# Two weight pieces split by one VectorE operation, from a ring of six places

## The chip, the cores and the metric

The kernel runs on one core of one Trainium2 chip. The metric is the device time of one execution in microseconds (us), the median over the runs shown. The profile tells of one execution, with its own time and its own span (first to last instruction). Engines are called by the names that the profile uses: PE is TensorE, PEld its weight loads, DVE is VectorE, ACT is ScalarE, POOL is GpSimd, and SP is the engine whose queue issues most of the transfers (DMAs).

## The reference, cut to what matters

The reference is a trunk of two decoder layers over 256 tokens of width 2048, in float32. Layer 0 mixes tokens by block-sparse attention, layer 1 by latent attention, and each is followed by the same gated MLP with 5632 inner features:

```python
def conv_glu_ffn(h, w_gate, w_up, conv_w, conv_b, w_down):
    g = h @ w_gate
    g = causal_depthwise_conv(g, conv_w, width=3) + conv_b
    return (jax.nn.silu(g) * (h @ w_up)) @ w_down

x = x + mixer_i(rms_norm(x, attn_norm[i]))
x = x + conv_glu_ffn(rms_norm(x, ffn_norm[i]), ...)
```

All weights are read once from the chip's main memory, 411 MB in all by the profile, and every product has to keep float32 accuracy.

## The kernel before

**Products in parts.** A float32 number is split into a high part (rounded to the format that TensorE multiplies, `fp32r`) and a low part (the rest). A product is three matmuls: high weights by high activations, high weights by low activations, low weights by high activations. Weights are worked on in *pieces* of 128x512 numbers (a few are 128x288 or 128x576). ACT makes the high part of a piece (`whi`, L183, a copy that rounds) and DVE the low part (`wlo`, L184, weight minus high part). PE then runs the piece's matmuls: twelve of 256 columns for a piece whose result has features in the partitions (`feat_major`, L402, L403, L404: four blocks, three matmuls each), six for a token-major piece (L376) and six for a *block* piece (L1181, L1182, L1183).

**The stream.** `Stream` brings the weights. A *unit* is 512 KB, two pieces in most places, in one of `AHEAD_UNITS = 6` buffers `raw`; at the split of unit u's first piece the loads up to unit u + 5 are recorded on SP's queue (L137, L141), the last of them into the buffer of unit u - 1, which it may fill once DVE has read the second piece there. The parts are in buffers of their own, five `whi` and five `wlo` (`AHEAD_PIECES + 1`). The program is one list of *quanta*, one for each piece. Ahead of quantum q it records the split of all pieces up to q + 3, then the matmuls of q, then the side work that hangs on q:

```python
ws.split(q + min(1 + q // 6, AHEAD_PIECES))
f(*args, *ws.take(q))
```

Each engine runs its own instructions in the recorded order. The split of piece i waits until PE has done with piece i - 5, whose buffers it takes. So ACT and DVE can be at most four pieces ahead of PE.

**The gated MLP.** 20 of the 44 feature tiles have their gate and up products from eight ordinary pieces; 24 have their gate products by *blocks*: four tiles together (a group, six groups a layer), in four rounds (kq) of seven block products. The weights for a round are loaded into `xroom` (L1140), which takes the place of the residual stream `xT`, kept in main memory meanwhile. Three of the seven are quarters of the loaded weights, and four are sums of these that DVE forms in `xroom` (`weight_sum`, L1159): t1 and t3, beside each other, are used by the block pieces s = 3 and 4, t2 and t4, beside each other, by s = 5 and 6. t2 and t4 lie where the group before had its result for a transpose by way of main memory (`turn`, L516, L518, L525), so the first t2 of a group waits for that transfer to have read it. Between block pieces stand ordinary pieces: up products and first down products, `BLOCK_EVERY = 2, 1, 1, 1, 2, 1, 1` of them after each.

When the last group is done, SP's queue issues in this place the reload of the down products kept so far (`a_back`, L1113, 2 MB) and of the residual stream (`xT`, L1134, four times 512 KB), between the loads of weight units.

**Side work.** DVE also evacuates the products from PSUM, multiplies, convolves and splits the activations (L1246, L1248, L1261, L1269, L1276); ACT scales, squares, applies the activation function and rounds (L1255, L1266, L1272). The buffers `nsq` (three) take squares for the norms.

Of the kernel before, what the change touches and what calls it, by code (L numbers as in the profile page):

```python
# [42 lines left out]
AHEAD_UNITS = 6  # L43
AHEAD_PIECES = 4

# [3 lines left out]
ROOM = 64  # L49
# [67 lines left out]
class Stream:  # L117
# [3 lines left out]
    def __init__(self, nc, raw_pool, part_pool, units, starts, pieces):  # L121
        self.starts = starts
        self.nc, self.raw_pool, self.part_pool = nc, raw_pool, part_pool
        self.units = units
        self.pieces = pieces
        self.raw, self.parts, self.after = {}, {}, {}
        self.loaded = self.split_to = 0

# [16 lines left out]
    def begin(self, load_x):  # L145
# [3 lines left out]
        ends = {1: 3, 3: 5, 5: 8, 8: 12, 11: 16}  # L149
# [14 lines left out]
    def split(self, upto):  # L164
        while self.split_to < min(upto, len(self.pieces)):
            i = self.split_to
            u, j, n = self.pieces[i]
            if u is None:
                b, c = BY_BLOCK
                w = j()  # L170
            else:
                self.load(u + AHEAD_UNITS)
                w = self.raw[u][:, j * n : (j + 1) * n]
                b, c = self.starts(u, j)
            hi = self.part_pool.tile([P, 512 + ROOM], F32R, name="whi")[:, b : b + max(n, 512)]
            lo = self.part_pool.tile([P, 512 + ROOM], F32R, name="wlo")[:, c : c + max(n, 512)]
            hi_, lo_ = hi[:, :n], lo[:, :n]
            if len(w.shape) == 4:
                hi_, lo_ = (x.rearrange("p (i j f) -> p i j f", i=2, j=2) for x in (hi_, lo_))
            if i == 0:  # L180
                self.nc.vector.tensor_copy(hi_, w)
            else:
                self.nc.scalar.copy(hi_, w)  # L183
            self.nc.vector.tensor_tensor(lo_, w, hi_.bitcast(F32), op=ALU.subtract)  # L184
            self.parts[i] = (hi, lo, n)
            self.split_to += 1
            for f, args in self.after.pop(i, ()):
                f(*args)

# [5 lines left out]
def trunk(ctx: ExitStack, tc: tile.TileContext, a, out):  # L195
# [4 lines left out]
    part_pool = ctx.enter_context(tc.tile_pool(name="parts", bufs=AHEAD_PIECES + 1))  # L200
# [25 lines left out]
    block_pieces = {}  # L226

    def gate_up_units(layer):
# [12 lines left out]
        for kind, *what in tokens:  # L241
            if kind == "block":
                block_pieces[(layer, *what)] = len(pieces)
                pieces.append((None, lambda layer=layer, what=what: blocks[layer].source(*what), 512))
            elif kind == "down":
                if at_ % 2 == 0:
# [6 lines left out]
                    downs_unit = len(units) - 1  # L253
                pieces.append((downs_unit, at_ % 2, 512))
                at_ += 1
            else:
                j, up, kq = what
                if kq % 2 == 0:
                    units.append(per[(2 * j + up) * 2 + kq // 2])
                    plain_unit = len(units) - 1  # L260
# [1637 lines left out]
```

## Time and profile before

| | |
|---|---|
| median of 3 runs | 2047.85 us (2047.83 to 2049.13) |
| the profiled execution | 2048.13 us, its span 2045.9 us |
| granted TensorE clock | 1.000 over the span |
| PE busy | 2037.8 us, 16300 instructions |
| DVE busy | 1660.1 us, 3211 instructions |
| ACT busy | 1290.9 us, 2474 instructions |
| MoBA attention, its output product | 0 to some 370 us |
| gated MLP of layer 0 | some 370 to 1065 us |
| latent attention, its output product | 1065 to some 1330 us |
| gated MLP of layer 1 | some 1330 to 2046 us |

How to read it: the duration of a matmul in the trace overlaps the next one's (a matmul of 256 columns is shown with 277 ns, while the next begins about 113 ns after it), so PE's share of busy time tells that it had something to do, and an idle time of PE is a wait that cost time. A row of the timeline has the start and the duration in us, the engine, the line, the operation, what it writes and reads, how many such operations follow each other, and in brackets the idle time of the engine ahead of it with what ended it. SPq is the queue in which SP issues transfers; their bytes move later. A row of a list of groups has the number of operations, their busy time in us, the mean ns of one, and the idle time ahead of them.

### The profile page before, as it was taken

How to read it: one execution, taken by the hardware profiler on the slowest of the kernel's cores; microseconds unless marked ns; L12 is line 12 of the kernel's file. 1: busy time of each engine (PE TensorE's matmuls, PEld its weight loads, DVE VectorE, ACT ScalarE, POOL GpSimd, SP SyncE). 2: the span in 40 equal slices, each digit the busy share in tenths (PEclk: the TensorE clock that was granted, in tenths of full speed). 3: DMA queues.
4: the chain of work that ended last, by engine and by line, in shares of the span. 5: the costliest groups of instructions: out<-in, count | busy, mean ns of one | idle time of the engine just before them, and what ended most of it. 6: DMA issues, size and time to landing. Idle time of an engine off the chain costs nothing.

```text
span 2045.9 us, 43563 instructions
## 1 busy us (share of the span) xinstructions
PE 2037.8 (100%) x16300; PEld 1970.4 (96%) x16300; DVE 1660.1 (81%) x3211; ACT 1290.9 (63%) x2474; POOL 48.7 (2%) x38
## 2 busy tenths in 40 slices
PE   9999999999999999999999999999999999999999
PEld 7888899999999999999999889999999999999999
DVE  7877777788998888888666998778889888898655
ACT  6656666666666666655556786666666666666443
POOL 0010000000000000000000110000000000000000
PEclk9999999999999999999999999999999999999999
DMA  7777776676766776676655646567666767758664
GB/s 274 235 250 223 226 231 210 211 233 203 225 218 207 237 239 189 223 267 208 199 196 159 210 152 183 189 214 234 207 214 217 227 217 227 225 186 301 202 211 129
DMA packets 162531, 440.35 MB, mean 215 GB/s; under 512 B 18816, under 2 KB 42880, under 8 KB 162064
## 3 DMA queue, kind: packets, MB, share of 16 engines
q1 hardware_dynamic: 162000, 437.21, 66.6%
q8 instruction: 127, 2.08, 0.4%
q14 instruction: 84, 0.69, 0.1%
q10 hardware_dynamic: 288, 0.33, 0.1%
q0 software_dynamic: 32, 0.04, 0.0%
HBM read 411.16 MB, written 26.35 MB: 214 GB/s over the span
## 4 chain that ended last, share of the span: by engine, by line
PE 97%; DVE 2%; ACT 0%; DMA 0%; issue 0%; SPq 0%; DVEq 0%; ACTq 0%
PE acc L404 23%; PE acc L403 22%; PE acc L402 22%; PE acc L376 16%; PE tp L1183 2%; PE tp L1181 2%; PE tp L1182 2%; PE sc L1183 2%; PE sc L1182 2%; PE sc L1181 2%; DVE wlo L184 1%; PE sc L657 0%; PE sc L656 0%; PE sc L655 0%; PE sc L758 0%; DMA xT<-in_xT 0%
## 5 line engine op out<-in xcount | busy, mean ns | idle before, releaser
L183 ACT CAST whi<-raw 128x512 fp32r<-128x512 f32 (+1 forms) x1271 | 775.6, 621 | 437.4 <-PE acc L403 223.4
L184 DVE TENSOR_TENSOR wlo<-raw,whi 128x512 fp32r<-128x512 f32 (+1 forms) x1272 | 861.1, 689 | 199.0 <-ACT whi L183 170.2
L404 PE MATMUL acc<-h,wlo 128*128 128x256 f32 x2112 | 585.3, 277 | 0.5 <-DVE wlo L184 0.5
L402 PE MATMUL acc<-h,whi 128*128 128x256 f32 x2112 | 585.1, 277 | 0.0
L403 PE MATMUL acc<-h,whi 128*128 128x256 f32 x2112 | 585.0, 277 | 0.0
L404 PEld LDWEIGHTS acc<-h,wlo 128*128 128x128 f32 x2112 | 396.5, 188 | 1.5 <-DVE wlo L184 1.4
L403 PEld LDWEIGHTS acc<-h,whi 128*128 128x128 f32 x2112 | 396.5, 188 | 0.0
L402 PEld LDWEIGHTS acc<-h,whi 128*128 128x128 f32 x2112 | 396.5, 188 | 0.0
L183 ACT CAST whi<-xroom 128x512 fp32r<-128x512 f32 x336 | 208.9, 622 | 102.6 <-PE acc L403 76.6
L376 PE MATMUL acc<-whi,h 128*128 128x512 f32 (+1 forms) x896 | 265.7, 377 | 0.9 <-ACT h L424 0.9
L184 DVE TENSOR_TENSOR wlo<-xroom,whi 128x512 fp32r<-128x512 f32 x336 | 231.1, 688 | 18.9 <-ACT whi L183 9.2
L376 PEld LDWEIGHTS acc<-whi,h 128*128 128x128 f32 x896 | 164.8, 188 | 31.1 <-ACT h L424 1.4
L376 PE MATMUL acc<-wlo,h 128*128 128x512 f32 (+1 forms) x448 | 168.8, 377 | 0.3 <-DVE wlo L184 0.2
L402 PE MATMUL acc<-oT,whi 128*128 128x256 f32 x512 | 142.8, 279 | 0.0
L403 PE MATMUL acc<-a_one,whi 128*128 128x256 f32 x512 | 142.0, 277 | 0.0
L404 PE MATMUL acc<-a_one,wlo 128*128 128x256 f32 x512 | 142.0, 277 | 0.0
L402 PE MATMUL acc<-a_one,whi 128*128 128x256 f32 x512 | 141.9, 277 | 0.0
L404 PE MATMUL acc<-oT,wlo 128*128 128x256 f32 x512 | 141.9, 277 | 0.0
L403 PE MATMUL acc<-oT,whi 128*128 128x256 f32 x512 | 141.8, 277 | 0.0
L402 PE MATMUL acc<-a_three,whi 128*128 128x256 f32 x512 | 141.3, 276 | 0.0
L403 PE MATMUL acc<-a_three,whi 128*128 128x256 f32 x512 | 141.3, 276 | 0.0
L404 PE MATMUL acc<-a_three,wlo 128*128 128x256 f32 x512 | 141.3, 276 | 0.0
(256 smaller groups left out, 3997.8 us busy)
## 6 DMA issues: line engine op xcount, KB each, us to landing
raw<-in_ffn_gu SPq DMA_DIRECT2D x256, 512.0 KB, 4.8
raw<-in_ffn_down SPq DMA_DIRECT2D x144, 512.0 KB, 4.8
xroom<-in_ffn_gu SPq DMA_DIRECT2D x192, 256.0 KB, 4.6
raw<-in_moba_wk SPq DMA_DIRECT2D x32, 512.0 KB, 5.8
raw<-in_moba_wv SPq DMA_DIRECT2D x32, 512.0 KB, 5.0
raw<-in_moba_wo SPq DMA_DIRECT2D x32, 512.0 KB, 4.8
raw<-in_ffn_down SPq DMA_DIRECT2D x64, 256.0 KB, 4.3
raw<-in_mla_wo SPq DMA_DIRECT2D x32, 512.0 KB, 3.8
```

What stands on the lines that cost most here:

```text
L183: self.nc.scalar.copy(hi_, w)
L184: self.nc.vector.tensor_tensor(lo_, w, hi_.bitcast(F32), op=ALU.subtract)
L376: mm(state["acc"][t][:, :n], src[:, kt, c : c + P], (t_lo if part == 1 else t_hi)[:, :n], start=kt == 0 and part == 0, stop=kt == k_last a ...
L402: mm(o, w_hi, src[:, kt, :S], start=first and k == 0, stop=False, skip_group_check=True)
L403: mm(o, w_hi, src[:, kt, S:], start=False, stop=False, skip_group_check=True)
L404: mm(o, w_lo, src[:, kt, :S], start=False, stop=kt == k_last, skip_group_check=True)
L1181: mm(o, x[:, 0], w_hi, start=opens and i == 0, stop=False, skip_group_check=True)
L1182: mm(o, x[:, 1], w_hi, start=False, stop=False, skip_group_check=True)
L1183: mm(o, x[:, 0], w_lo, start=False, stop=last and i == 1, skip_group_check=True)
```

## The change

The low parts of two pieces of the gated MLP are formed by one DVE operation over 128x2x512 numbers.

- `mates` names the pairs: the two pieces of a unit of gate, up or down weights; the block pieces s = 3 and 4 (t1 and t3); s = 5 and 6 (t2 and t4). There are 264 pairs in a layer, 528 in all. The pieces of a pair may have other pieces between them in PE's order. All other pieces (attention, output products, block pieces s = 0 to 2) are split one by one as before.
- When the first piece of a pair is to be split, ACT rounds both, one after the other, and then DVE forms both low parts. When the second piece's turn comes, there is nothing left to do.
- The parts lie in one tile `whi` and one tile `wlo` with six places each, of 512 + 64 numbers. A pair takes the two places whose pieces were the longest out of use, so its two halves may be one to five places apart. A place is taken only when the piece in it was used by an earlier quantum.
- `AHEAD_UNITS` is 5 instead of 6. `nsq` has two buffers instead of three.
- At the start, the last part of `x` is loaded behind the tenth piece instead of the twelfth.

The order of the matmuls on PE is the same. Names moved by some lines: L184 is L213 now, L183 is L203, L1159 is L1200.

```diff
@@ -40,13 +40,14 @@
 G_Q, G_K, G_QR, G_KR = 0, 32, 64, 128
 G_END = 192
 
-AHEAD_UNITS = 6
+AHEAD_UNITS = 5
 AHEAD_PIECES = 4
+SLOTS = 6
 
 SINGLE_UNITS = 8
 WO_OPEN = 8
 
-ROOM = 64
+SLOT = 512 + 64
 
 BY_TOKEN, BY_FEATURE, BY_BLOCK = (8, 8), (24, 56), (24, 24)
 
...
@@ -118,13 +119,18 @@
 
 
 
-    def __init__(self, nc, raw_pool, part_pool, units, starts, pieces):
-        self.starts = starts
+    def __init__(self, nc, raw_pool, part_pool, units, starts, pieces, mates):
+        self.starts, self.mates = starts, mates
         self.nc, self.raw_pool, self.part_pool = nc, raw_pool, part_pool
         self.units = units
         self.pieces = pieces
         self.raw, self.parts, self.after = {}, {}, {}
         self.loaded = self.split_to = 0
+        self.high, self.low = (
+            part_pool.tile([P, SLOTS * SLOT], F32R, name=name).rearrange("p (k c) -> p k c", c=SLOT)
+            for name in ("whi", "wlo")
+        )
+        self.last_use = [-1] * SLOTS
 
     def load(self, upto):
         while self.loaded < min(upto, len(self.units)):
...
@@ -146,7 +152,7 @@
 
 
 
-        ends = {1: 3, 3: 5, 5: 8, 8: 12, 11: 16}
+        ends = {1: 3, 3: 5, 5: 8, 8: 12, 9: 16}
         load_x(0, 1)
         at = 1
         for u in range(AHEAD_UNITS):
...
@@ -161,31 +167,50 @@
                     at = end
         self.loaded = AHEAD_UNITS
 
-    def split(self, upto):
+    def raw_of(self, i):
+        u, j, n = self.pieces[i]
+        if u is None:
+            return j()
+        self.load(u + AHEAD_UNITS)
+        return self.raw[u][:, j * n : (j + 1) * n]
+
+    def split(self, upto, now):
         while self.split_to < min(upto, len(self.pieces)):
             i = self.split_to
-            u, j, n = self.pieces[i]
-            if u is None:
-                b, c = BY_BLOCK
-                w = j()
-            else:
-                self.load(u + AHEAD_UNITS)
-                w = self.raw[u][:, j * n : (j + 1) * n]
-                b, c = self.starts(u, j)
-            hi = self.part_pool.tile([P, 512 + ROOM], F32R, name="whi")[:, b : b + max(n, 512)]
-            lo = self.part_pool.tile([P, 512 + ROOM], F32R, name="wlo")[:, c : c + max(n, 512)]
-            hi_, lo_ = hi[:, :n], lo[:, :n]
-            if len(w.shape) == 4:
-                hi_, lo_ = (x.rearrange("p (i j f) -> p i j f", i=2, j=2) for x in (hi_, lo_))
-            if i == 0:
-                self.nc.vector.tensor_copy(hi_, w)
-            else:
-                self.nc.scalar.copy(hi_, w)
-            self.nc.vector.tensor_tensor(lo_, w, hi_.bitcast(F32), op=ALU.subtract)
-            self.parts[i] = (hi, lo, n)
+            if i not in self.parts:
+                self.split_these(i, now)
             self.split_to += 1
             for f, args in self.after.pop(i, ()):
                 f(*args)
+
+    def split_these(self, i, now):
+        u, _, n = self.pieces[i]
+        b, c = BY_BLOCK if u is None else self.starts(*self.pieces[i][:2])
+        mate, both = self.mates.get(i, (None, None))
+        these = [i] if mate is None else [i, mate]
+        slots = sorted(sorted(range(SLOTS), key=lambda k: self.last_use[k])[: len(these)])
+        w = [self.raw_of(k) for k in these]
+        for k, slot, src in zip(these, slots, w):
+            assert self.last_use[slot] < now
+            self.last_use[slot] = k
+            hi, lo = self.high[:, slot, b : b + max(n, 512)], self.low[:, slot, c : c + max(n, 512)]
+            hi_ = hi[:, :n]
+            if len(src.shape) == 4:
+                hi_ = hi_.rearrange("p (i j f) -> p i j f", i=2, j=2)
+            if i == 0:
+                self.nc.vector.tensor_copy(hi_, src)
+            else:
+                self.nc.scalar.copy(hi_, src)
+            self.parts[k] = (hi, lo, n)
+        if mate is None:
+            hi, lo, _ = self.parts[i]
+            hi, lo, src = hi[:, :n], lo[:, :n], w[0]
+            if len(src.shape) == 4:
+                hi, lo = (x.rearrange("p (i j f) -> p i j f", i=2, j=2) for x in (hi, lo))
+        else:
+            two = slice(slots[0], slots[1] + 1, slots[1] - slots[0])
+            hi, lo, src = self.high[:, two, b : b + n], self.low[:, two, c : c + n], both()
+        self.nc.vector.tensor_tensor(lo, src, hi.bitcast(F32), op=ALU.subtract)
 
     def take(self, i):
         return self.parts.pop(i)
...
@@ -197,7 +222,7 @@
     const = ctx.enter_context(tc.tile_pool(name="const", bufs=1))
     keep = ctx.enter_context(tc.tile_pool(name="keep", bufs=1))
     raw_pool = ctx.enter_context(tc.tile_pool(name="raw", bufs=AHEAD_UNITS))
-    part_pool = ctx.enter_context(tc.tile_pool(name="parts", bufs=AHEAD_PIECES + 1))
+    part_pool = ctx.enter_context(tc.tile_pool(name="parts", bufs=1))
     small = ctx.enter_context(tc.tile_pool(name="small", bufs=4))
     ps_acc = ctx.enter_context(tc.tile_pool(name="ps_acc", bufs=4, space=PSUM))
     ps_tp = ctx.enter_context(tc.tile_pool(name="ps_tp", bufs=2, space=PSUM))
...
@@ -241,6 +266,9 @@
         for kind, *what in tokens:
             if kind == "block":
                 block_pieces[(layer, *what)] = len(pieces)
+                if what[2] in (4, 6):
+                    k = block_pieces[(layer, *what[:2], what[2] - 1)]
+                    mates[k] = len(pieces), lambda layer=layer, i=what[2] - 4: blocks[layer].totals(i)
                 pieces.append((None, lambda layer=layer, what=what: blocks[layer].source(*what), 512))
             elif kind == "down":
                 if at_ % 2 == 0:
...
@@ -251,6 +279,9 @@
                         src = [down[u][:, c : c + 512] for u, c in ((u0, c0), (u1, c1))]
                     units.append((src, 2, 512))
                     downs_unit = len(units) - 1
+                    first_piece = len(pieces)
+                else:
+                    mates[first_piece] = len(pieces), lambda u=downs_unit: whole(u)
                 pieces.append((downs_unit, at_ % 2, 512))
                 at_ += 1
             else:
...
@@ -258,8 +289,14 @@
                 if kq % 2 == 0:
                     units.append(per[(2 * j + up) * 2 + kq // 2])
                     plain_unit = len(units) - 1
+                    first_piece = len(pieces)
+                else:
+                    mates[first_piece] = len(pieces), lambda u=plain_unit: whole(u)
                 pieces.append((plain_unit, kq % 2, 512))
         return pieces
+
+    def whole(u):
+        return ws.raw[u].rearrange("p (i c) -> p i c", i=2)
 
     def pieces_of(units):
         done = list(fixed)
...
@@ -285,7 +322,7 @@
             return 0, 0
         return BY_TOKEN if u < 96 or tok_units <= u < tok_units + 44 else BY_FEATURE
 
-    ws = Stream(nc, raw_pool, part_pool, units, starts, pieces_of(units))
+    ws = Stream(nc, raw_pool, part_pool, units, starts, pieces_of(units), mates)
 
 
     att = ExitStack()
...
@@ -1125,6 +1162,7 @@
             room = keep.tile([P, KD * S], F32, name="xroom", tag="xT")
             self.rawq = [room[:, i * 1024 : (i + 1) * 1024] for i in range(2)]
             self.wsum = [room[:, (4 + i) * 512 : (5 + i) * 512] for i in range(4)]
+            self.both = room.rearrange("p (i c) -> p i c", c=512)[:, 4:]
             self.turn = room[:, 6 * 512 :]
 
         def leave_room(self, kq):
...
@@ -1146,6 +1184,9 @@
 
         def total(self, i):
             return self.wsum[i].rearrange("p (i j f) -> p i j f", i=2, j=2)
+
+        def totals(self, i):
+            return self.both[:, i : i + 2]
 
         def source(self, g, kq, s):
             if s < 3:
...
@@ -1718,13 +1759,13 @@
 
 
     assert len(quanta) == len(ws.pieces), (len(quanta), len(ws.pieces))
-    ws.split(1)
+    ws.split(1, 0)
     for f, args in side.pop(-1):
         f(*args)
     for q, (f, args) in enumerate(quanta):
         for g, gargs in ahead.pop(q, []):
             g(*gargs)
-        ws.split(q + min(1 + q // 6, AHEAD_PIECES))
+        ws.split(q + min(1 + q // 6, AHEAD_PIECES), q)
         f(*args, *ws.take(q))
         for g, gargs in (*leading.get(q, ([], []))[0], *leading.pop(q, ([], []))[1], *side.pop(q, [])):
             g(*gargs)
```

More of the change, by code (lines that the diff above doesn't have):

```diff
@@ L225, in trunk @@
     units += units_of("moba_wo")
-    block_pieces = {}
+    block_pieces, mates = {}, {}
     def gate_up_units(layer):
@@ L441, in square @@
             else:
-                self.sq[j] = small.tile([P, S], F32, name="nsq", bufs=3)
+                self.sq[j] = small.tile([P, S], F32, name="nsq", bufs=2)
                 nc.scalar.activation(self.sq[j], xT[:, j, :], AF.Square)
@@ L1500, in cq_part @@
         else:
-            sq = small.tile([P, S], F32, name="nsq", bufs=3)
+            sq = small.tile([P, S], F32, name="nsq", bufs=2)
             nc.scalar.activation(sq, src, AF.Square)
```

## Prediction

> **What bounds the kernel now.** I read the page's busy times first, then the waits of PE, the groups of DVE and ACT, and the timelines of the places where cover is thin.
>
> ```profile
> PE 2037.8 (100%) x16300; PEld 1970.4 (96%) x16300; DVE 1660.1 (81%) x3211; ACT 1290.9 (63%) x2474; POOL 48.7 (2%) x38
> 370.00:950.00 580.00, 579.50 (x5076) 578.77 (x5075) 503.56 (x907) 376.07 (x692) 1.09 (x1) 1.00 0.69 223
> L404 PE MATMUL acc<-h,wlo 128*128 128x256 f32 x2112 | 585.3, 277 | 0.5 <-DVE wlo L184 0.5
> PE acc L376 <- DVE wlo L184: 0.2, 1, 0.2
> PEld acc L376 <- DVE wlo L184: 2.3, 6, 0.5
> PEld acc L404 <- DVE wlo L184: 1.4, 5, 0.7
> L184 DVE TENSOR_TENSOR wlo<-raw,whi 128x512 fp32r<-128x512 f32 x1256 | 849.2, 688 | 198.6 <-ACT whi L183 169.8 <-PE tp L1182 9.7 <-PE sc L1182 8.8
> L184 DVE TENSOR_TENSOR wlo<-raw,whi 128x576 fp32r<-128x576 f32 x16 | 11.9, 753 | 0.4 <-ACT whi L183 0.4
> L183 ACT CAST whi<-raw 128x512 fp32r<-128x512 f32 x1255 | 765.3, 620 | 434.5 <-PE acc L403 223.4 <-DVE wlo L184 110.9 <-PE acc L376 38.5
> ```
>
> PE is idle for 8.1 of 2045.9 us, and in the blocks of layer 0's MLP (second row: us, PE, PEld, DVE, ACT, POOL, clock, share of the DMA engines, GB/s) for 0.5 of 580. The clock is granted in full. What the low parts cost PE today is 0.5 + 0.2 + 2.3 + 1.4 = 4.4 us at most, so no cheaper way of forming them can gain more than that by the waits, and the change is to be judged by the cover that it takes away. DVE works 503.56 of those 580 us: in the block stretch it is close to being a second bound. The order of PE's matmuls doesn't change.
>
> **The operation itself.** 64 more numbers cost 753 - 688 = 65 ns, so 1024 numbers take about 688 + 512 x 65/64 = 1.21 us, against twice 0.688 = 1.38. In a full queue operations follow each other faster than they last:
>
> ```profile
> 442.51 0.69 DVE L1159 TENSOR_TENSOR xroom<-xroom 128x512 f32<-128x512 f32 x1
> 443.11 0.68 DVE L184 TENSOR_TENSOR wlo<-xroom,whi 128x512 fp32r<-128x512 f32 x1
> 443.71 0.69 DVE L184 TENSOR_TENSOR wlo<-raw,whi 128x512 fp32r<-128x512 f32 x1
> 444.31 0.69 DVE L184 TENSOR_TENSOR wlo<-xroom,whi 128x512 fp32r<-128x512 f32 x1
> 444.98 0.28 PE L402 MATMUL acc<-h,whi 128*128 128x256 f32 x1
> 445.09 0.28 PE L403 MATMUL acc<-h,whi 128*128 128x256 f32 x1
> 445.22 0.28 PE L404 MATMUL acc<-h,wlo 128*128 128x256 f32 x1
> 445.33 0.28 PE L402 MATMUL acc<-h,whi 128*128 128x256 f32 x1
> ```
>
> Starts are 0.60 us apart, so a pair holds the queue for 0.60 + 0.52 = 1.12 us where two operations hold it for 1.20: 0.08 us for each of 528 pairs, 42 us of DVE's time over the run. All of it lies beside PE's work. The price is on the other side: the first low part of a pair, which PE needs first, is there 0.52 us later than alone, and later by one more rounding on ACT (0.62 us) where that is the last to come.
>
> The Trainium skill (VectorE: DVE Perf Modes, The DRAIN you can't avoid) says that the next operation doesn't start until the pipe is empty; by it a pair would save its whole fixed part, 1.38 - 1.21 = 0.17 us, and DVE 90 us. The rows above, 0.60 apart at 0.69 each, don't show that, and the sum goes by them.
>
> **First place: one raw buffer less, at the reload of the residual.** SP's queue behind the last group of layer 0, before:
>
> ```order
> L141 DMA raw<-in_ffn_gu 128x1024
> L1113 DMA a_back<-part 128x4096
> L141 DMA raw<-in_ffn_gu 128x1024
> L1134 DMA xT<-kept 128x1024
> L141 DMA raw<-in_ffn_gu 128x1024
> L1134 DMA xT<-kept 128x1024
> L141 DMA raw<-in_ffn_gu 128x1024
> L1134 DMA xT<-kept 128x1024
> L141 DMA raw<-in_ffn_gu 128x1024
> L1134 DMA xT<-kept 128x1024
> L141 DMA raw<-in_ffn_gu 128x1024 x3
> L141 DMA raw<-in_ffn_down 128x1024 x3
> ```
>
> and now:
>
> ```order
> L147 DMA raw<-in_ffn_gu 128x1024
> L1150 DMA a_back<-part 128x4096
> L147 DMA raw<-in_ffn_gu 128x1024
> L1172 DMA xT<-kept 128x1024
> L147 DMA raw<-in_ffn_gu 128x1024
> L1172 DMA xT<-kept 128x1024
> L147 DMA raw<-in_ffn_gu 128x1024
> L1172 DMA xT<-kept 128x1024
> L147 DMA raw<-in_ffn_gu 128x1024
> L1172 DMA xT<-kept 128x1024
> L147 DMA raw<-in_ffn_gu 128x1024 x4
> L147 DMA raw<-in_ffn_down 128x1024 x3
> ```
>
> Eight gate and up units stand behind `a_back` where seven stood: each place in the queue now brings the unit before, so the unit that went ahead of those 2 MB goes behind them.
>
> ```profile
> 895.28 0.38 SPq L141 DMA_DIRECT2D raw<-in_ffn_gu  x1
> 895.75 0.38 SPq L1113 DMA_DIRECT2D a_back<-part  x1
> 896.19 0.42 SPq L141 DMA_DIRECT2D raw<-in_ffn_gu  x1
> 897.50 0.57 SPq L141 DMA_DIRECT2D raw<-in_ffn_gu  x1
> 895.50:921.50 26.00, 26.00 (x232) 26.00 (x232) 18.19 (x36) 13.99 (x27) 0.00 (x0) 1.00 1.00 381
> 903.83 0.62 ACT L183 CAST whi<-raw 128x512 fp32r<-128x512 f32 x1 [0.73 <-PE acc L403]
> 908.78 1.15 ACT L183 CAST whi<-raw 128x512 fp32r<-128x512 f32 x2 [2.96 <-DMA raw<-in_ffn_gu]
> 912.50 0.62 ACT L183 CAST whi<-raw 128x512 fp32r<-128x512 f32 x1 [2.25 <-DMA raw<-in_ffn_gu]
> 915.05 0.62 ACT L183 CAST whi<-raw 128x512 fp32r<-128x512 f32 x1 [0.92 <-DMA raw<-in_ffn_gu]
> 909.37 0.28 PE L404 MATMUL acc<-h,wlo 128*128 128x256 f32 x1
> ```
>
> The DMA engines are full here (share 1.00), transfers land in the order of their issue, and ACT already waits for three units in turn; the four pieces of cover hide it. Counted in the recorded order, the unit issued at 895.28 was rounded from 903.83, and its first low part used by PE at 909.37, four pieces of twelve matmuls later. A matmul takes 580 / 5076 = 0.114 us in the second row above, so units are used 24 x 0.114 = 2.7 us apart. Now it lands when the unit of 896.19 landed, and is rounded at 908.78: both pieces until 909.93, their low parts from 910.0 to 911.2, 1.9 us behind PE's 909.37. The next has its roundings from 912.50 to 913.65 and its low parts at 914.9; PE would want them at 909.37 + 2.7 + 1.9 = 914.0, so 0.9 more. The third, from 915.05, is ready at 917.5, when PE, 2.8 late, wants it at 917.6. From there on landings are 2.5 us apart, and PE doesn't fall further back. **2.8 us.** SP's later loads wait for buffers that are freed later, but behind a full queue.
>
> In layer 1 the same place has more cover:
>
> ```profile
> 1866.34 1.15 ACT L183 CAST whi<-raw 128x512 fp32r<-128x512 f32 x2 [1.75 <-DMA raw<-in_ffn_gu]
> 1868.13 0.28 PE L404 MATMUL acc<-h,wlo 128*128 128x256 f32 x1
> ```
>
> The unit used at 1868.13 is rounded from 1866.34, ready at 1868.8: **0.7 us**. Bounds for both: nothing, if PE's cover is longer than I read it, and 2.7 us (a unit) in each at most beyond the sum, if a whole unit more is late.
>
> **Second place: where DVE waits for the cross transfer.** At the opening of layer 0's last group DVE's order was
>
> ```order
> L1159 TENSOR_TENSOR xroom<-xroom 128x512
> L1269 TENSOR_TENSOR c<-c,acc 128x256
> L184 TENSOR_TENSOR wlo<-raw,whi 128x512
> L184 TENSOR_TENSOR wlo<-xroom,whi 128x512
> L1159 TENSOR_TENSOR xroom<-xroom 128x512
> L184 TENSOR_TENSOR wlo<-raw,whi 128x512
> L1159 TENSOR_TENSOR xroom<-xroom 128x512
> L1276 TENSOR_TENSOR a_three<-c,a_three 128x256
> L184 TENSOR_TENSOR wlo<-xroom,whi 128x512
> ```
>
> and is
>
> ```order
> L1200 TENSOR_TENSOR xroom<-xroom 128x512
> L1310 TENSOR_TENSOR c<-c,acc 128x256
> L213 TENSOR_TENSOR wlo<-xroom,whi 128x512
> L1200 TENSOR_TENSOR xroom<-xroom 128x512
> L213 TENSOR_TENSOR wlo<-raw,whi 128x2x512
> L1200 TENSOR_TENSOR xroom<-xroom 128x512
> L1317 TENSOR_TENSOR a_three<-c,a_three 128x256
> L213 TENSOR_TENSOR wlo<-xroom,whi 128x2x512
> ```
>
> The first raw low part between the sums is gone (it is made with its mate, further ahead), and the two behind the second sum are pairs now.
>
> ```profile
> 819.27 0.69 DVE L1159 TENSOR_TENSOR xroom<-xroom 128x512 f32<-128x512 f32 x1 [1.79 <-DMA there<-xroom]
> 819.88 0.68 DVE L184 TENSOR_TENSOR wlo<-raw,whi 128x512 fp32r<-128x512 f32 x1
> 820.62 0.39 PE L404 MATMUL acc<-h,wlo 128*128 128x256 f32 x1 [0.51 <-DVE wlo L184]
> 822.16 0.39 PE L1183 MATMUL sc<-wlo,a_sums 128*128 128x256 f32 x1
> DVE xroom L1159 <- DMA there<-xroom: 8.5, 7, 1.8
> ```
>
> The sum waits 1.79 us for the transfer, and everything behind it starts from 819.88, whoever is ready. The pair ends at 821.1 instead of 820.56, and PE, waiting already, waits 0.53 longer. The next pair stands behind a sum and `a_three` (0.60 + 0.33), so it runs from 821.93 to 823.15, against 822.16 + 0.53: 0.46 more. So 1.0 us at the longest of the seven such waits; at the shortest the cover eats it. With a mean of 8.5 / 7 = 1.2 us for a wait, I take 0.4 each, **3 us** (bounds 0 and 7).
>
> **Third place: pairs that pile up inside a round.** At 445.22 (rows above) PE uses a low part that was ready at 444.40, 0.82 ahead. In the new order two pairs stand in this place (s = 3 and 4, then two ordinary pieces) instead of the two operations at 443.11 and 443.71: the second is ready 2 x 0.52 later, less some 0.1 that earlier pairs saved, at about 445.3. With the 0.06 that a semaphore takes that is 0.1 to 0.3 late. There are 48 rounds; in most the cover in the trace is over 1 us and holds. I take six with 0.25, **1.5 us** (bounds 0 and 12).
>
> The rest: in the attention stages nothing is paired, and one raw buffer less takes a unit of cover (2.7 us) from loads that mostly land earlier than that; latent attention and the start, where they don't, get **0.5** (bounds 0 and 2). Two `nsq` buffers and the earlier part of `x` are covered by the same four pieces: nothing; the waits above are what it would cost. Against it, shorter queues on DVE give back some of the 4.4 us: **-0.5** (bounds -4.4 and 0).
>
> The sum: 2.8 + 0.7 + 3 + 1.5 + 0.5 - 0.5 = 8.0 us, on 2048.13 us of the profiled execution, which is 0.28 above the median of the runs: 2047.85 + 8.0 = 2055.9, so **2056 us**.
>
> **The rivals.**
>
> *The cover holds (22%).* DVE has 42 us less to do, so its queue is emptier at each of these places than I count, and what is late for ACT is not late for PE. For it: in the trace ACT waits 2.96 us for a unit and PE for none. Against it: at 909.37 and 820.62 the sums leave no cover. Time: 2048 to 2051, most of it the 0.7 to 2.8 us of the reload.
>
> *It is faster (4%).* The low part of a second piece is always there by the time PE comes to it, and PE's first matmul of such a piece need not wait. Place: the waits of PE and PEld for `wlo`, 4.4 us in all, of which perhaps half sit at second pieces, and the opening of an ordinary piece behind a block piece, whose first three matmuls take 445.33 - 444.98 = 0.35 us instead of 3 x 0.114 = 0.34: 0.01 us at half of the 528 second pieces. Price: -2.2 - 2.6 = -4.8, so 2043. It decides only if no raw unit is late and the wait itself, not the change of operands, is what these matmuls pay for.
>
> *The clock drops (4%).* PE's first matmuls show two rates:
>
> ```profile
> 1.19 4.23 PE L303 MATMUL sc<-zeros 128*128 128x512 bf16 x12 [1.19 <-DVE zeros L300]
> 11.74 36.81 PE acc L376 x161
> ```
>
> Twelve in 4.23 us are 0.35 each, while 512 columns later take 36.81 / 161 = 0.23 (second row, of the chain of work): some 3 us of the opening ran at half speed. Were the idle time at the reload to bring that back, 3 us at half speed would lose 1.5 us in each layer: 2059. Against it: PE idles there in two parts of 1.9 and 0.9, and idle times near 1 us cost no clock in this trace. The Trainium skill (TensorE: Matmul & The Clock Gate, What's actually happening) puts the window at about 3.4 us of idleness; no run here shows it yet.
>
> *The pairs are worse than counted (8%).* DVE, at 87% in the block stretch, has its pairs wait for two roundings in most rounds, idles, and doesn't catch up: 12 of 48 rounds with 0.5 and 7 us at the cross transfers: 2066.
>
> **How the numbers follow.** My sum has 62%, with 2052 to 2063 of its own. The change is slower in all cases but the first two; faster or slower by 0.2% means by 4.1 us here, what a measurement can tell. That gives slower 0.72, within 0.2% 0.24, faster 0.04. The range for 8 in 10 runs from 2048, where the cover holds, to 2063.
>
> **What would show it.** Right: PE idles some 2 us near 909 and 0.5 to 1 near 1868 for `wlo` whose rounding waited for a raw unit; the wait of L404 and L1183 for `wlo` (L213) grows from 0.5 to 4 or more; pairs last 1.21 us. Wrong: no wait of PE over 1 us behind the reload; low parts of pairs early everywhere; or the time between matmuls, 0.114 us, changes, which I take as fixed.

## The result, and the profile after

The changed kernel takes 2074.59 us, the median of 4 runs (2073.46 to 2077.57), beside 2048.23 us of the kernel before in the same comparison: 1.013 times as long, 95% interval 1.0113 to 1.0148, 26.4 us more. The forecast was slower by 8.0 us; its sign is right, and its size and its range (2048 to 2063) are not. The profiled execution of the changed kernel took 2077.57 us, with a span of 2075.3; it is the longest of the four, so what is read from its trace adds up to 3 us more than the medians tell.

Line numbers below are those of each kernel; in the changed one the rounding is L203, the low part L213, the feature-major matmuls (gate and up pieces among them) L439 to L441, the token-major ones L413, the square `nsq` L480 and its sum `nacc` L484. Busy times, from the page after:

```profile
PE 2051.1 (99%) x16300; PEld 1975.8 (95%) x16300; DVE 1613.5 (78%) x2683; ACT 1267.4 (61%) x2474; POOL 47.8 (2%) x38
```

The change does what it says: DVE has 3211 - 2683 = 528 operations and 46.6 us less. PE, which sets the end, is now idle for 2075.3 - 2051.1 = 24.2 us instead of 8.1, and busy 13 us longer for the same 16300 matmuls. Its waits, and one of ACT (what waited for what: us in total, times, longest):

```profile
PE acc L441 <- DVE wlo L213: 8.1, 9, 1.3
PE tp L508 <- DVE nacc L484: 2.5, 1, 2.5
PE acc L439 <- ACT whi L203: 2.5, 2, 1.4
PE sc L1224 <- DVE wlo L213: 0.6, 2, 0.4
ACT nsq L480 <- DVE nacc L484: 7.6, 10, 1.7
ACT whi L203 <- DMA raw<-in_mla_wqn: 4.2, 1, 4.2
```

The wait of L441 (L404 before) was 0.5 and is 8.1, the largest; the wait of `tp` for the sum of the squares is new; and ACT waits 7.6 us for that sum. The matmuls of the block pieces (L1224), at which the forecast put part of its largest term, wait 0.6.

Part of the longer busy time of PE is its clock. Two stretches at the end of the first norm and two at the reload in layer 0 (columns: window, us, busy time and count of PE, PEld, DVE, ACT and POOL, granted clock, DMA share, GB/s), changed kernel:

```profile
50.00:54.00 4.00, 1.51 (x8) 1.12 (x7) 2.35 (x5) 2.48 (x5) 0.00 (x0) 0.77 0.58 184
54.00:60.00 6.00, 6.00 (x17) 4.70 (x18) 2.65 (x15) 1.33 (x3) 3.32 (x3) 0.58 0.44 142
924.00:927.00 3.00, 1.45 (x6) 1.25 (x7) 2.10 (x3) 2.25 (x5) 0.00 (x0) 0.83 1.04 422
927.00:930.00 3.00, 3.00 (x18) 3.00 (x17) 1.83 (x3) 1.90 (x5) 0.00 (x0) 0.60 1.03 410
```

and the kernel before, where PE doesn't idle ahead of it:

```profile
54.00:60.00 6.00, 6.00 (x28) 4.95 (x28) 5.85 (x18) 3.42 (x7) 0.00 (x0) 1.00 0.55 170
```

Where the time was lost can be read by setting the start of the n-th matmul after against that of the n-th before, as PE's order is the same in both. The difference grows by 7.9 us between 42 and 52 us (squares of the first norm), by 3.6 at the opening of layer 0's MLP (390 to 432) and 3.7 at that of layer 1 (1350 to 1392), by 0.6 and 0.5 at the ends of the two norms ahead of them (near 382 and 1341), by 4.8 and 4.0 at the two reloads (from 909 and from 1868), by 1.9 in latent attention (1144 to 1150), and by 2.4 in the rounds in between, in steps of 0.3 to 0.8. The clock has a part in this: it stands at 0.50 for 6.83 us behind the first norm and for 3.41 us behind the reload of layer 0, which costs half of these times at most, 5.1 us.

### The profile page after: what moved, and what is told of

Read it like the earlier page. It is cut to its first block, busy times and chain, and to the rows that moved or that the text cites. A ratio compares the mean times of both kernels' runs of the same rounds, so it can differ in the third digit from the quotient of the medians.

```text
span 2075.3 us, 42448 instructions
## 1 busy us (share of the span) xinstructions
PE 2051.1 (99%) x16300; PEld 1975.8 (95%) x16300; DVE 1613.5 (78%) x2683; ACT 1267.4 (61%) x2474; POOL 47.8 (2%) x38
## 4 chain that ended last, share of the span: by engine, by line
PE 82%; issue 6%; DVE 6%; DMA 3%; ACT 2%; POOL 0%; SPq 0%; POOLq 0%; ACTq 0%; DVEq 0%
PE acc L441 19%; PE acc L439 19%; PE acc L440 19%; PE acc L413 12%; DVE wlo L213 3%; PE tp L1224 2%; PE tp L1223 2%; PE tp L1222 2%; DMA raw<-in_ffn_gu 2%; PE sc L1224 2%; PE sc L1223 1%; PE sc L1222 1%; ACT whi L203 1%; DMA raw<-in_moba_wq 0%; DMA raw<-in_mla_wqn 0%
## 5 line engine op out<-in xcount | busy, mean ns | idle before, releaser
L203 ACT CAST whi<-raw 128x512 fp32r<-128x512 f32 (+1 forms) x1271 | 751.2, 619 | 417.8 <-PE acc L440 259.8
L213 DVE TENSOR_TENSOR wlo<-raw,whi 128x1024 fp32r<-128x1024 f32 (+2 forms) x840 | 798.2, 962 | 261.6 <-ACT whi L203 251.6
L441 PE MATMUL acc<-h,wlo 128*128 128x256 f32 x2112 | 588.0, 278 | 8.5 <-DVE wlo L213 8.0
L439 PE MATMUL acc<-h,whi 128*128 128x256 f32 x2112 | 586.2, 278 | 2.5 <-ACT whi L203 2.5
L441 PEld LDWEIGHTS acc<-h,wlo 128*128 128x128 f32 x2112 | 397.2, 188 | 11.7 <-DVE wlo L213 11.1
L439 PEld LDWEIGHTS acc<-h,whi 128*128 128x128 f32 x2112 | 397.2, 188 | 2.9 <-ACT whi L203 2.9
L413 PE MATMUL acc<-whi,h 128*128 128x512 f32 (+1 forms) x896 | 268.1, 380 | 1.2 <-ACT h L461 0.7
L203 ACT CAST whi<-xroom 128x512 fp32r<-128x512 f32 x336 | 205.6, 620 | 102.3 <-PE acc L440 63.9
L213 DVE TENSOR_TENSOR wlo<-xroom,whi 128x512 fp32r<-128x512 f32 (+1 forms) x240 | 215.5, 898 | 26.8 <-ACT whi L203 25.4
L413 PEld LDWEIGHTS acc<-whi,h 128*128 128x128 f32 x896 | 166.1, 189 | 32.4 <-ACT whi L203 1.3
L413 PE MATMUL acc<-wlo,h 128*128 128x512 f32 (+1 forms) x448 | 170.3, 380 | 0.5 <-DVE wlo L213 0.4
L439 PE MATMUL acc<-oT,whi 128*128 128x256 f32 x512 | 142.8, 279 | 0.0
L441 PE MATMUL acc<-a_one,wlo 128*128 128x256 f32 x512 | 142.1, 278 | 0.3 <-DVE wlo L213 0.2
L439 PE MATMUL acc<-a_one,whi 128*128 128x256 f32 x512 | 141.9, 277 | 0.0
L441 PE MATMUL acc<-oT,wlo 128*128 128x256 f32 x512 | 141.9, 277 | 0.0
L441 PE MATMUL acc<-a_three,wlo 128*128 128x256 f32 x512 | 141.3, 276 | 0.0
L439 PE MATMUL acc<-a_three,whi 128*128 128x256 f32 x512 | 141.3, 276 | 0.0
```

What stands on the lines that cost most here:

```text
L203: self.nc.scalar.copy(hi_, src)
L213: self.nc.vector.tensor_tensor(lo, src, hi.bitcast(F32), op=ALU.subtract)
L413: mm(state["acc"][t][:, :n], src[:, kt, c : c + P], (t_lo if part == 1 else t_hi)[:, :n], start=kt == 0 and part == 0, stop=kt == k_last a ...
L439: mm(o, w_hi, src[:, kt, :S], start=first and k == 0, stop=False, skip_group_check=True)
L441: mm(o, w_lo, src[:, kt, :S], start=False, stop=kt == k_last, skip_group_check=True)
```

## The experiments

The change has three parts that can be undone alone: two `nsq` buffers, five raw buffers, and the pairs (with the ring that carries them). Each kernel was timed beside the kernel before, which took 2048.1 to 2048.6 us in these comparisons.

**Two nsq buffers alone**, in the kernel before:

```diff
-self.sq[j] = small.tile([P, S], F32, name="nsq", bufs=3)
+self.sq[j] = small.tile([P, S], F32, name="nsq", bufs=2)
-sq = small.tile([P, S], F32, name="nsq", bufs=3)
+sq = small.tile([P, S], F32, name="nsq", bufs=2)
```

> The kernel before with two nsq buffers instead of three, nothing else. Theory 'three causes' (two nsq buffers, one raw buffer less, and the pairs each cost time of their own): the squares of the first norm wait for the sums on DVE near 44 to 50 us, PE stands idle some 2.6 us there, its clock drops behind that, and with 0.8 us near 382 the run is some 8 us longer: 2056 to 2057 us. Rival 'the pairs alone' (the prediction on record counts two nsq buffers at nothing): 2048 to 2049 us, and the wait for the sums is seen only where pairs fill DVE's queue.

Measured: 2054.34 us, ratio 1.0033 (1.0020 to 1.0045), +6.2. The forecast's "nothing" for it falls. It is less than the 8 us that I expected here: in this trace nothing is lost at the end of the norm near 382. Timeline of this run:

```profile
46.67 0.69 DVE L184 TENSOR_TENSOR wlo<-raw,whi 128x512 fp32r<-128x512 f32 x1 [1.05 <-ACT whi L183]
47.28 0.88 DVE L447 TENSOR_TENSOR nacc<-nacc,nsq 128x256 f32<-128x256 f32 x2
47.79 0.42 ACT L443 ACTIVATE nsq<-xT 128x256 f32<-128x256 f32 x1 [1.15 <-DVE nacc L447]
48.12 0.60 ACT L183 CAST whi<-raw 128x512 fp32r<-128x512 f32 x1
48.75 0.69 DVE L184 TENSOR_TENSOR wlo<-raw,whi 128x512 fp32r<-128x512 f32 x1 [0.59 <-ACT whi L183]
53.40 0.58 PE L471 MATMUL tp<-ones,nacc 128*128 128x1 f32 x4 [2.45 <-DVE nacc L447]
```

A loop between two engines: the sum on DVE (47.28) stands behind a low part; the next square on ACT (47.79) waits for that sum, since both buffers are taken; the rounding on ACT (48.12) stands behind the square; and the next low part on DVE (48.75) waits for the rounding. Neither engine can run ahead of the other any more, all the work that shares their queues falls to the pace of this loop, and PE waits 2.45 us for the last sum. There are no pairs in this kernel, so it isn't they that make the sum late. The profile before had the sign of it, in a row of ACT's waits that the forecast didn't read:

```profile
ACT nsq L443 <- DVE nacc L447: 2.1, 4, 0.8
```

With three buffers ACT already waited four times for a buffer to come free: there was little slack to take.

**Five raw buffers alone**, in the kernel before:

```diff
-AHEAD_UNITS = 6
+AHEAD_UNITS = 5
-ends = {1: 3, 3: 5, 5: 8, 8: 12, 11: 16}
+ends = {1: 3, 3: 5, 5: 8, 8: 12, 9: 16}
```

> The kernel before with five raw buffers instead of six, nothing else. Theory 'three causes': nearly all that the changed kernel lost at the two reloads of the residual (4.6 and 3.7 us) and in latent attention (2.1) is here: 2057 to 2059 us. The sum on record has 2.8 + 0.7 + 0.5 = 4.0 for it: 2052 us. Rival 'the pairs alone': raw units arrive late for ACT only, PE keeps its cover without pairs: 2048 to 2050 us.

Measured: 2052.96 us, the median of 10 runs (2050.73 to 2055.20), ratio 1.0023 (1.0014 to 1.0032), +4.8. That is nearer to the 4.0 of the forecast's sum than to the 9 to 11 that I expected by then: most of the loss at the reloads needs something else as well. The profiled run, which was the fastest and shows 2.6 of the 4.8 us, lost 1.1 us at the reload of layer 0, nothing at layer 1's, and 2.3 in latent attention, where ACT now waits 4.3 us for one unit of `mla_wqn` (2.2 before).

**No pairs**, in the changed kernel, ring, five raw and two nsq buffers kept:

```diff
-mate, both = self.mates.get(i, (None, None))
+mate = both = None
```

> The changed kernel (ring of six places, five raw buffers, two nsq buffers) with each low part formed alone again, so that only the pairs are left out. Theory 'three causes': the start (8 us) and most of the reloads and latent attention (8 to 10 us) stay, and the openings of the two MLPs (3.7 and 4.2 us) and the waits in the rounds (2.5 us) go: 2064 to 2067 us. Rival 'the pairs alone': 2048 to 2051 us.

Measured: 2060.38 us, ratio 1.0060 (1.0046 to 1.0073). So the pairs cost 2074.59 - 2060.38 = 14.2 us, over half of the whole, and neither 'the pairs alone' nor my lower price for them holds. The intervals of the two ratios are far apart.

**Both buffer changes, no ring**, in the kernel before (the two diffs above together):

> The kernel before with two nsq buffers and five raw buffers, its five places of a pool kept: the changed kernel without pairs and without the ring. If the two add and the ring costs nothing: 2048.1 + 6.2 + 4.8 = 2059.1, 2058 to 2061 us, level with the run without pairs (2060.4). If the ring of six places in one tile costs something of its own: 2056 us or less. If the ring's sixth place helps: 2062 us or more.

Measured: 2058.90 us, ratio 1.0051 (1.0037 to 1.0065). The parts add: 2048.1 + 6.2 + 4.8 = 2059.1. The ring without pairs stands 1.5 us above, within the intervals, so no cost of its own is shown. Measured one by one, 6.2 + 4.8 + 14.2 = 25.2 of the 26.4 us are accounted for, and the rest lies within the intervals.

**Three nsq buffers**, in the changed kernel:

```diff
-self.sq[j] = small.tile([P, S], F32, name="nsq", bufs=2)
+self.sq[j] = small.tile([P, S], F32, name="nsq", bufs=3)
...
-ms = small.tile([P, NT], F32, name="ms")
+ms = small.tile([P, NT], F32, name="ms", bufs=1)
```

and so on: the second `nsq` like the first, and fewer copies of six other small statistics.

> The changed kernel with three nsq buffers again (the room is taken from spare copies of small statistics), pairs and five raw buffers kept. Theory 'three causes': the 7.8 us of the start and some 1.4 us at the ends of the norms are given back, the clock near 50 to 60 us is full: 2065 to 2067 us. Rival 'the pairs alone' (PE waits there because DVE is late through the change as a whole): 2073 to 2075 us, the idle time only moves.

Measured: 2067.38 us, ratio 1.0092 (1.0078 to 1.0106), 7.2 less than the changed kernel, as the first experiment says from the other side. The granted clock from 54 to 60 us is 1.00 here.

**Why pairs cost.** First the order of the change with separate low parts: both roundings on ACT, then two operations of 512.

```diff
-else:
-    two = slice(slots[0], slots[1] + 1, slots[1] - slots[0])
-    hi, lo, src = self.high[:, two, b : b + n], self.low[:, two, c : c + n], both()
-self.nc.vector.tensor_tensor(lo, src, hi.bitcast(F32), op=ALU.subtract)
+for k, src in zip(these, w):
+    hi, lo, _ = self.parts[k]
+    hi, lo = hi[:, :n], lo[:, :n]
+    ...
+    self.nc.vector.tensor_tensor(lo, src, hi.bitcast(F32), op=ALU.subtract)
```

> The changed kernel with its order kept (both roundings of a pair on ScalarE, then the low parts), but the low parts formed by two operations of 512 again. Theory 'the pair waits' (what the pairs cost, 14 us between the run without pairs, 2060.4, and the changed kernel, 2074.6, comes from the one operation: its first half is ready only after the second rounding and 0.5 us later): 2060 to 2063 us, and no stalls of 1.3 us at the openings of the MLPs. Rival 'the order' (the second rounding, pulled ahead by one piece, is what makes ScalarE and VectorE late for the token sums): 2069 to 2075 us, with the stalls at the openings still there.

Measured: 2059.49 us, ratio 1.0057 (1.0044 to 1.0069). The order costs nothing that shows here; the one operation does. Then the same with the low part of the second piece ahead of the first's:

```diff
-for k, src in zip(these, w):
+for k, src in zip(these[::-1], w[::-1]):
     hi, lo, _ = self.parts[k]
```

> As the run with two low parts for a pair, but the low part of the second piece is formed before that of the first. So the first piece's low part is ready as late as in the changed kernel, behind both roundings and 1.2 us of VectorE, and no operation is wider than 512. Theory 'lateness' (what costs is only when the first low part is ready): back to the changed kernel's 2071 to 2076 us, with its stalls of 1.3 us at the openings. Rival 'the wide operation' (1024 columns over two places cost of themselves): 2059 to 2063 us, as with two low parts in order.

Measured: 2079.05 us, ratio 1.0149 (1.0135 to 1.0163). No operation is wider than 512 here, and the loss is back, with 4.5 us on top. So it is the lateness of the first low part that costs, and not the width. How much of it is the second rounding and how much the 0.5 us of the longer operation was not separated. In the waits of PE the gate and up pieces have this row with separate low parts in order:

```profile
PE acc L438 <- DVE wlo L210: 0.4, 2, 0.2
```

and this one with the order reversed:

```profile
PE acc L438 <- DVE wlo L210: 9.6, 13, 1.4
```

The opening of layer 0's MLP in the changed kernel, where the sums of the tokens are made (timeline, rows of three engines in order of time):

```profile
413.03 1.14 ACT L203 CAST whi<-raw 128x512 fp32r<-128x512 f32 x2
414.19 1.23 DVE L213 TENSOR_TENSOR wlo<-raw,whi 128x1024 fp32r<-128x1024 f32 x1 [1.73 <-ACT whi L203]
415.34 0.42 DVE L1289 TENSOR_TENSOR g<-acc,rstd_b 128x256 f32<-128x256 f32 x1
416.39 0.42 DVE L1125 TENSOR_TENSOR a_mix<-a_mix 128x256 f32<-128x256 f32 x1
416.85 0.51 ACT L1109 ACTIVATE a_mix<-xT,par 128x256 f32<-128x256 f32 x1 [2.38 <-DVE a_mix L1125]
417.26 1.12 ACT L203 CAST whi<-raw 128x512 fp32r<-128x512 f32 x2
418.42 1.23 DVE L213 TENSOR_TENSOR wlo<-raw,whi 128x1024 fp32r<-128x1024 f32 x1 [0.94 <-ACT whi L203]
419.70 0.39 PE L441 MATMUL acc<-h,wlo 128*128 128x256 f32 x1 [1.11 <-DVE wlo L213]
```

The same loop as at the squares, with other links: DVE waits 1.73 us for the two roundings, the step of the token sum (416.39) stands behind the pair, ACT waits 2.38 us for that step before it goes on with the tokens and the next two roundings, and the next pair waits for both of them. In each turn the pair adds its second rounding and 0.5 us, and PE is 1.11 us short at 419.70. ACT's waits for this step grow, before and in the changed kernel:

```profile
ACT a_mix L1072 <- DVE a_mix L1088: 8.7, 6, 1.7
ACT a_mix L1109 <- DVE a_mix L1125: 14.3, 6, 2.4
```

Without pairs, with the same buffers, they are 8.8 us. With separate low parts in the same order DVE waits less:

```profile
411.94 1.29 DVE L210 TENSOR_TENSOR wlo<-raw,whi 128x512 fp32r<-128x512 f32 x2 [1.21 <-ACT whi L203]
415.71 1.29 DVE L210 TENSOR_TENSOR wlo<-raw,whi 128x512 fp32r<-128x512 f32 x2 [0.42 <-ACT whi L203]
```

**Where pairs cost.** No pairs at the two openings:

```diff
-else:
+elif (layer, 0, 0, 0) in block_pieces:
     mates[first_piece] = len(pieces), lambda u=plain_unit: whole(u)
```

> The changed kernel, but the 44 gate and up pieces ahead of the first round of blocks in each layer are formed alone: 44 of 528 pairs are left out. Theory 'the place' (pairs cost at the openings, where the token sums tie ScalarE and VectorE to each other, 3.7 us in each layer): 7 us less than the changed kernel, 2066 to 2068 us. Rival 'evenly' (each pair costs the same, 14.2 / 528 = 0.027 us): 1.2 us less, 2073 to 2074 us. If the lost time only moves on to the rounds behind: 2072 to 2075 us.

Measured: 2065.67 us, ratio 1.0088 (1.0074 to 1.0102), 8.9 less than the changed kernel for 44 of 528 pairs. 'Evenly' is out. By the starts of the matmuls in the two traces, 8.4 us less is lost at the openings and the ends of the norms ahead of them, and 3.9 less at the reloads behind, which are reached at other times (the two profiled executions are 13.2 us apart).

Pairs of block sums alone (both `mates[first_piece] = ...` taken out):

> The changed kernel with pairs only for the block sums (96 of 528); gate, up and down pieces are formed alone. Theory 'the place': without the openings and without pairs behind the reloads what is left over the run without pairs (2060.4) is part of the 2.5 us of the rounds: 2061 to 2063 us. Rival 'evenly': 96 x 0.027 = 2.6 us, 2063 us. If the block pairs are what delays the token sums and the reload: over 2066 us.

Measured: 2062.44 us, ratio 1.0067 (1.0054 to 1.0080), 2.1 over the run without pairs, which the two intervals don't tell from none. What is left, 2065.67 - 2062.44 = 3.2 us (the two intervals just overlap), belongs to the gate, up and down pairs behind the openings; by the starts of the matmuls in the traces of these last two kernels, 1.8 us is lost with them at the first reload and 1.4 at the second. So the pairs and the missing raw buffer meet there. In the changed kernel:

```profile
916.73 1.14 ACT L203 CAST whi<-raw 128x512 fp32r<-128x512 f32 x2 [3.68 <-DMA raw<-in_ffn_gu]
923.60 1.14 ACT L203 CAST whi<-raw 128x512 fp32r<-128x512 f32 x2 [5.42 <-DMA raw<-in_ffn_gu]
924.27 0.38 PE L439 MATMUL acc<-h,whi 128*128 128x256 f32 x1 [1.40 <-ACT whi L203]
926.05 0.58 PE L441 MATMUL acc<-h,wlo 128*128 128x256 f32 x1 [1.28 <-DVE wlo L213]
```

The unit that lands at 923.6 is late for PE's first matmul, and then its pair, behind both roundings, is late once more for the low part.

**Cover against buffers.** Five raw buffers and one place more for the pieces, in the kernel before (with the small statistics and the loads of the start as in the experiments above, and three nsq buffers):

```diff
-AHEAD_UNITS = 6
-AHEAD_PIECES = 4
+AHEAD_UNITS = 5
+AHEAD_PIECES = 5
```

> The kernel before with five raw buffers, six part buffers and five pieces of cover instead of four, three nsq buffers kept (room from spare copies of small statistics). If cover in pieces is worth as much as a raw buffer: the 4.8 us of five raw buffers come back, 2048 to 2050 us. If a unit that lands late is late for either: 2051 to 2055 us. Faster than before, 2046 or less, if the six places also shorten the waits at the cross transfers.

Measured: 2048.66 us, the median of 11 runs, ratio 1.0000 (0.9991 to 1.0009). A fifth piece of cover (a sixth place, and splits recorded one piece earlier) gives back all that the raw buffer cost. And the opposite:

```diff
-AHEAD_UNITS = 6
-AHEAD_PIECES = 4
+AHEAD_UNITS = 7
+AHEAD_PIECES = 3
```

> The kernel before with seven raw buffers, four part buffers and three pieces of cover. If raw units are what runs short at the reload and in latent attention: 2044 to 2048 us. If the cover of four pieces is what hides the waits of VectorE for the cross transfers and the token sums, as the pairs showed, those places cost 0.6 us or more each: over 2055 us.

Measured: 2062.22 us, ratio 1.0068 (1.0055 to 1.0080). Three pieces of cover are too few, in many small places: PE's waits for low parts become

```profile
PE acc L404 <- DVE wlo L184: 3.3, 10, 0.4
PE acc L376 <- DVE wlo L184: 2.3, 8, 0.6
```

**Pairs with the buffers of before:**

```diff
-AHEAD_UNITS = 5
-SLOTS = 6
+AHEAD_UNITS = 6
+SLOTS = 5
...
+if mate is not None and sorted(self.last_use)[1] >= now:
+    mate = None
```

and three nsq buffers and the loads of the start as before.

> Pairs with the buffers of before: a ring of five places, six raw and three nsq buffers; a pair is formed only where two places are free, else its pieces are formed alone (some 370 of 528 pairs are left). Theory 'lateness at places': the openings (7 to 9 us) and part of the rounds (2 us) stay, the pairs behind the reloads cost little since the units land earlier: 2055 to 2060 us. If pairs pay once no buffer is taken for them: 2048 or less. If waiting for two free places of five makes the roundings late everywhere: over 2065 us.

Measured: 2066.35 us, ratio 1.0085 (1.0071 to 1.0099), above what I expected. Its groups of pairs (out of raw units, and of block sums; count, busy time and mean ns behind the shapes):

```profile
L215 DVE TENSOR_TENSOR wlo<-raw,whi 128x1024 fp32r<-128x1024 f32 x384 | 469.6, 1223 | 253.0 <-ACT whi L205 233.8 <-PE sc L1225 8.6 <-PE tp L1225 4.1
L215 DVE TENSOR_TENSOR wlo<-xroom,whi 128x1024 fp32r<-128x1024 f32 x48 | 58.7, 1222 | 2.3 <-PE tp L1225 1.6
```

and the row of PE's waits:

```profile
PE acc L443 <- DVE wlo L215: 9.1, 15, 1.2
```

There were 384 + 48 = 432 pairs, not 370. They cost 17.8 us with six raw and three nsq buffers in place. By the starts of the matmuls, 4.3 us are lost at each of the two openings and 0.7 at the end of each norm, a little more than in the changed kernel, 6.2 in the rounds (2.4 in the changed kernel), and 0.7 at the reloads. What the ring of five places, of which a pair takes two at once, adds to the pairs themselves was not separated. It does show that with a ring of five the pairs don't pay with the buffers given back. No version tried is faster than the kernel before.

## Why the prediction was wrong, by its own steps

- **What bounds the kernel, and what the edit can gain:** right. PE's waits for low parts were the most that could be gained, and the change is indeed judged by the cover that it takes away.
- **The operation itself:** right in its time, too high in what it saves. A pair of 1024 was put at 1.21 us and takes 1.22 (the groups above), and the next operation follows 415.34 - 414.19 = 1.15 us behind, where 1.12 was counted. DVE's busy time fell by 46.6 us, which looks like the 42 of the rows, but 20 of them are there without pairs: the run without pairs, with the same buffers and ring, has 1640.2, so the pairs themselves saved 26.7 us. That is less than the 42. The drain rule of the Trainium skill (VectorE: DVE Perf Modes, The DRAIN you can't avoid) would give 90; the same paragraph lets an operation that isn't held start earlier, and the starts 0.60 us apart agree with that.
- **First place, one raw buffer less (2.8 + 0.7 at the reloads, with the pair counted in, and 0.5 in latent attention):** right in the wait of layer 0 and too small elsewhere. PE waits 1.40 us for a rounding and 1.28 for a low part at the reload of layer 0, 2.7 in all beside 2.8; but the clock then falls to 0.50 for 3.41 us, which the sum had left to a rival, and the reload loses 4.8. In layer 1 the "more cover" did not hold: 1.08, 1.28 and 0.74 us of waits, 4.0 lost instead of 0.7. Both reloads together lost 8.8 instead of 3.5, latent attention 1.9 instead of 0.5. That one raw buffer alone, without pairs, measured 4.8 (2.9 to 6.6 by the interval), near the 4.0 of these terms, is luck: it lost 1.1 at the reloads and 2.3 in latent attention.
- **Second and third place (3 and 1.5 us at the cross transfers and in the rounds):** right in kind, too high at the cross transfers. Both together gave 2.4 us by the starts of the matmuls, not 4.5. At the transfer worked out in the forecast (820) 0.5 us is lost, and 0.4 is gained ahead of it, where DVE's wait for the transfer is 1.39 us instead of 1.79.
- **"Two `nsq` buffers ... are covered by the same four pieces: nothing":** this step failed; it measured 6.2 us. Cover in pieces hides a delay that happens once. It does not hide a loop in which ACT waits for DVE and DVE for ACT at each turn, since each turn eats some of it.
- **What the sum left out:** this step failed too, and it is the largest: the openings of the MLPs, 8.9 us by the run without pairs there, and 8.4 in their own place by the traces. I looked for thin cover where the profile before shows PE or ACT waiting (820, 909) and in one round at 445, and not where ACT and DVE wait for each other while PE is covered. The rule that the first low part of a pair is there 0.52 us later, and later by one more rounding, was on record and right; it was applied at the reloads, the cross transfers and the rounds, and not at the openings.
- **The give-back of 0.5:** none is seen in PE's waits.
- **The rivals:** 'the clock drops' (4%) had the price about right (1.5 us; 3.41 us at 0.50 cost 1.7 at most) and the place in part: it came at the reload of layer 0, not at that of layer 1, and behind the first norm, which it did not name. 'The pairs are worse than counted' (8%, 2066; its terms add up to some 2065) had the mechanism, DVE waiting for two roundings, and put it in the rounds, not at the openings. The bounds for nothing-terms were not carried into the range: with an upper end for the squares and for the openings it would have reached the result.

## What to carry to other kernels

When one operation takes the place of two, ask when its first half is needed and where two engines already wait for each other; there the lateness comes back at each turn, however long the queue of ready work is. Before a buffer is taken away, look for the waits of the engine that fills it, even where PE doesn't wait: a short wait that repeats (here 2.1 us in four times) says that little slack is left. And a piece of cover that is ready for PE can be worth as much as a raw buffer of nearly the same size, as five raw buffers with six places show.

## What was not expected of the hardware

The granted clock fell behind shorter idle time than I had reckoned with. A single wait of 2.5 us for the sum of the squares was accompanied or followed by reduced clock in seven of the eight profiles that have it, in the changed kernel from 52.2 us on, inside the wait. (Four matmuls of one column follow the wait, so between matmuls of 512 columns PE has next to nothing to do for 3.1 to 3.5 us.) The mean clock from 54 to 60 us is 0.58 in the changed kernel, 0.72 with two nsq buffers alone, and 0.50 with separate low parts. In the run without pairs it was 1.00 behind the same wait:

```profile
54.00:60.00 6.00, 6.00 (x28) 4.94 (x27) 4.48 (x18) 3.85 (x8) 3.73 (x3) 1.00 0.50 171
```

In the reload of layer 0, two waits of 1.40 and 1.28 us within 2 us of each other were enough for 0.60; in layer 1, 1.08 and 1.28 were not. The clock itself is either 1.00 or 0.50 in these traces, and the falls last 3.41 or 6.83 us: in the changed kernel it is 1.00 again from 60 us and from 930 us on.

The traces also show what decides. In all 14 of them the stretches between two changes of the clock are whole multiples of 3.413 us (47.79, 51.20, 6.83 and 3.41 among them). On that grid I estimate how much of each 3.413 us PE's matmuls fill, from their starts, at 0.23 us for one of 512 columns and 0.114 for one of 256. The ten falls all come at the end of a stretch that is filled to 0.38 or less; of the other stretches at full clock, some 8,400 in the 14 traces, none is filled to less than 0.40. In the run without pairs the grid cuts the same gap in two, 0.40 and 0.49, and the clock stays. In the changed kernel the reload of layer 0 has both waits in one stretch, 0.11; that of layer 1 doesn't, 0.48. So a gap of this length costs clock or not by where it falls on the grid.

The Trainium skill (TensorE: Matmul & The Clock Gate, What's actually happening) puts the window at about 3.4 us and lets the clock fall after an idle one; the length agrees with the 3.413 us of the traces, but the windows ahead of the falls here were not idle, so for that the measured rows decide.
